# State-space stage: each slab's PSUM bank is copied to SBUF, and GpSimd's tap is added first

## The chip, the cores and the metric

The kernel runs on one core of a Trainium2 chip. The core has five engines with an instruction queue of its own each: TensorE (matrix products into PSUM), VectorE, ScalarE and GpSimd (elementwise work; GpSimd reads and writes SBUF alone here) and SyncE (starts the DMAs). An engine takes its instructions strictly in order, and semaphores hold an instruction until what it needs is done. The metric is the device time of one execution in microseconds; less is better.

## The reference

Two transformer-like blocks on a sequence of 256 tokens of width 1024 in float32. The first has a sparse-attention mixer and a state-space mixer (Mamba-2 style), each followed by a feed-forward layer with a causal convolution; the second has a gated delta rule with memory attention and a feed-forward layer. What the change touches is the state-space mixer's entry:

```python
proj = h @ w_in
z = proj[..., :SSD_D_INNER]
xbc = jax.nn.silu(causal_dwconv(proj[..., SSD_D_INNER:SSD_D_INNER + SSD_CONV_DIM], conv_w, conv_b))
...
y = ssd_scan(x_ssm, dt, a, bm, cm) + d_skip.astype(f32)[:, None] * x_ssm
y = y.reshape(b, s, SSD_D_INNER) * jax.nn.silu(z.astype(f32))
```

The convolution runs over positions, with four taps per channel and a bias; x (2048 channels), B and C (512 each) go through it, z (2048) does not.

## The kernel before, in words

The stages run one after the other: attention, feed-forward 0, state space, feed-forward 1, delta rule, feed-forward 2. Activations lie feature-major, 128 features on the partitions by 256 positions. A weight slab of 256 output features comes by two DMAs of 512 KB; each half is split into a high part (ScalarE, L361, whi) and a low part (VectorE or GpSimd, L362, wlo), and every product is three matmuls of such parts (L308). `up` gathers one slab's products in a PSUM bank of 128 x 512 numbers, two feature tiles of 256 positions (tag u, two banks; tag b, two more, serves all small products; four acc banks), and then calls that slab's `evac`.

The state-space stage has 20 slabs: B and C (two each), x (eight, x00 to x31) and z (eight). B0 and C0 are the two slabs that `enter` makes while it comes from the stage before; their results lie in acc banks. In this stage x.rb is None (the normalisation is already in the activations), so `scaled` (L744) hands on the bank itself. For B, C and x the evac is `convsilu`, which calls `conv` (L753): per feature tile c, ScalarE writes u = tap 3 times the bank plus bias (L762), and tap 2 times the bank to a scratch tile called tap (L764); VectorE adds taps 1 and 0 with a shift of two and three positions, each a scalar_tensor_tensor that reads the bank and u (L767); and GpSimd adds the scratch tile with a shift of one (L769). Then `silu2` (L771): th = tanh(u/2) on ScalarE (L773), out = (th + 1) u on VectorE (L774); the factor of two is taken out later. For z the evac is `gate`: silu2 of the bank itself.

TensorE's order is written by hand (the order of the Python code, with `fill` and `need` putting slabs between the small products of the scan). VectorE, ScalarE and GpSimd are ordered by a scheduler at build time from priorities; `high_priority(offset=URGENT // 2)` moves an instruction forward. At the entry `enter` transposes B0 and C0 back, and then `tails` makes the 32 dt columns: matmuls, a copy to SBUF by ScalarE (L681, tail), two transposes by TensorE; from them come dt, softplus (L781 to L792) and da. After that TensorE runs slabs z00, x00, x01, then the first small products of the scan: decay sums, ah (L1206), and per pair of heads dd (L1245), ee (L1247 to L1249), w (L1251) and x (L1261, which reads a b bank).

Of the kernel before, what the change touches and what calls it, by code (L numbers as in the profile page):

```python
# [10 lines left out]
F32 = mybir.dt.float32  # L11
# [7 lines left out]
P = 128  # L19
S = 256  # L20
# [12 lines left out]
URGENT = 2000  # L33
# [214 lines left out]
class Net:  # L248
# [492 lines left out]
            self.need("tail")  # L741
        return x

    def scaled(self, pool, ps, rb, tag="p", bufs=2):  # L744

        if rb is None:
            return ps.rearrange("p (c s) -> p c s", c=2)
        p = pool.tile([P, 2, S], F32, tag=tag, name=self.nm(tag), bufs=bufs)
        with self.tc.high_priority(offset=URGENT // 2):
            self.nc.vector.tensor_tensor(p, ps.rearrange("p (c s) -> p c s", c=2), rb[:, None, :].to_broadcast([P, 2, S]), op=ALU.mult)  # L750
        return p

    def conv(self, u, p, w, i, taps, bias=None, pool=None):  # L753

        nc = self.nc
        col = lambda c, t: self.pc(w, i[c] * taps + t)
        both = range(len(u))
        for c in both:
            if bias is None:
                nc.scalar.activation(u[c], p[c], AF.Copy, scale=col(c, taps - 1))  # L760
            else:
                nc.scalar.activation(u[c], p[c], AF.Identity, scale=col(c, taps - 1), bias=self.pc(bias, i[c]))  # L762
            if pool is not None:
                nc.scalar.activation(pool[c], p[c], AF.Copy, scale=col(c, taps - 2))  # L764
        for c in both:
            for sh in range(1 if pool is None else 2, taps):
                nc.vector.scalar_tensor_tensor(u[c][:, sh:], p[c][:, :S - sh], col(c, taps - 1 - sh), u[c][:, sh:], op0=ALU.mult, op1=ALU.add)  # L767
            if pool is not None:
                nc.gpsimd.tensor_add(u[c][:, 1:], u[c][:, 1:], pool[c][:, :S - 1])  # L769

    def silu2(self, out, u, th):  # L771

# [60 lines left out]


    def ffn(self, i, conv, left, gain_pre, mem=None):
        nc = self.nc
        with self.tc.tile_pool(name=f"ffn{i}", bufs=3) as fp:
# [304 lines left out]
    def ssd(self, left):  # L1142
        nc = self.nc
        mm = self.mm
        with self.tc.tile_pool(name="ssd", bufs=1) as sp:
            t = lambda s, shape, dt=F32, b=1: sp.tile(shape, dt, tag=s, name=self.nm(s), bufs=b)
            out = {}

            def convsilu(key, i, b=1):

                def evac(ps, x):
                    p = self.scaled(sp, ps, x.rb)
                    u, o = t("u", [P, 2, S], b=2), t(key if b == 1 else key[0], [P, 2, S], b=b)
                    pool = [self.np_.tile([P, S], F32, tag="sq", name=self.nm("tap"), bufs=3) for _ in range(2)]
                    self.conv((u[:, 0], u[:, 1]), (p[:, 0], p[:, 1]), "scw", (i, i + 1), 4, "scb", pool)
                    self.silu2(o, u, t("th", [P, 2, S], b=2))
                    out[key] = o
                return evac

            def gate(key):  # L1160
                def evac(ps, x):
                    u, o = self.scaled(sp, ps, x.rb), t("z", [P, 2, S], b=4)
                    self.silu2(o, u, t("th", [P, 2, S], b=2))
                    out[key] = o
                return evac

# [3 lines left out]
            x = self.enter(left, None, "gain10", "ssd_up", [convsilu("B0", 16), convsilu("C0", 20)], ("ssd_dt", 32),  # L1170
                           then=lambda x: (setattr(self, "pool_lo", POOL_E), self.add("z00", zs(0, 0, x))))
# [18 lines left out]
            ps = self.bank()  # L1190
# [10 lines left out]
            ps = self.bank()  # L1201
# [90 lines left out]
            for g in range(4):  # L1292
# [18 lines left out]
                for c in range(2):  # L1311
                    ps = self.bank()
# [599 lines left out]
```

## Time and profile before

| | |
|---|---|
| time before, median of 3 runs | 1330.9 us (1323.39 to 1338.49) |
| the profiled execution: time, span | 1329.81 us, 1328.0 us |
| TensorE busy, whole span | 1246.6 us (94%) |
| VectorE, ScalarE, GpSimd busy | 896.1, 715.9, 226.9 us |
| mean granted TensorE clock | 0.964 of full speed |

The profile is of one execution. In its rows PE is TensorE's matmuls and PEld its weight loads, DVE is VectorE, ACT ScalarE, POOL GpSimd. Times are us from the start of the span, and "out<-in" names the tiles; L is the line in the kernel. Consecutive instructions of an engine overlap by about 0.1 us in the rows. The waits are inferred from semaphore events: where several semaphores are awaited, the last counts.

### The profile page before, as it was taken

How to read it: one execution, taken by the hardware profiler on the slowest of the kernel's cores; microseconds unless marked ns; L12 is line 12 of the kernel's file. 1: busy time of each engine (PE TensorE's matmuls, PEld its weight loads, DVE VectorE, ACT ScalarE, POOL GpSimd, SP SyncE). 2: the span in 40 equal slices, each digit the busy share in tenths (PEclk: the TensorE clock that was granted, in tenths of full speed). 3: DMA queues.
4: the chain of work that ended last, by engine and by line, in shares of the span. 5: the costliest groups of instructions: out<-in, count | busy, mean ns of one | idle time of the engine just before them, and what ended most of it. 6: DMA issues, size and time to landing. Idle time of an engine off the chain costs nothing.

```text
span 1328.0 us, 22701 instructions
## 1 busy us (share of the span) xinstructions
PE 1246.6 (94%) x8874; PEld 1110.1 (84%) x8874; DVE 896.1 (67%) x1647; ACT 715.9 (54%) x1340; POOL 226.9 (17%) x149
## 2 busy tenths in 40 slices
PE   8999989999999989999899999998867999999997
PEld 8874579999988888877899998888867887999996
DVE  6776658877776677865798777577873335755554
ACT  6365547765556655544766655743423454744442
POOL 2000003110005322411211000350321332300000
PEclk9997999999999989989999999987878899999999
DMA  8740136655544334424455555342311114555551
GB/s 316 283 143 1 33 118 201 197 184 188 183 153 140 118 110 143 137 102 140 167 194 191 181 181 187 116 155 96 112 48 49 64 64 159 172 192 180 185 184 41
DMA packets 54108, 192.78 MB, mean 145 GB/s; under 512 B 6128, under 2 KB 6768, under 8 KB 53616
## 3 DMA queue, kind: packets, MB, share of 16 engines
q1 hardware_dynamic: 54000, 191.32, 43.2%
q8 instruction: 70, 1.15, 0.4%
q14 instruction: 38, 0.31, 0.1%
HBM read 190.25 MB, written 1.05 MB: 144 GB/s over the span
## 4 chain that ended last, share of the span: by engine, by line
PE 49%; DVE 9%; issue 7%; ACT 3%; POOL 2%; DMA 0%; POOLq 0%; DVEq 0%; ACTq 0%
PE u L308 29%; PE acc L308 16%; PE b L308 3%; DVE u L767 2%; DVE wlo L362 1%; ACT whi L361 1%; PE b L313 1%; POOL wlo L362 1%; POOL x L1267 0%; POOL rs L457 0%; DVE et L1698 0%; DVE rs L459 0%; POOL l2r L1585 0%; DMA raw<-in_gdn_up_dram 0%; ACT u L762 0%
## 5 line engine op out<-in xcount | busy, mean ns | idle before, releaser
L361 ACT ACTIVATE whi<-raw 128x1024 fp32r<-128x1024 f32 (+1 forms) x342 | 356.1, 1048 | 255.9 <-PE u L308 122.2
L308 PE MATMUL u<-xhi,whi 128*128 128x256 f32 x1600 | 467.0, 292 | 12.3 <-DVE xp L1628 5.5
L362 DVE TENSOR_TENSOR wlo<-raw,whi 128x1024 fp32r<-128x1024 f32 (+1 forms) x283 | 351.3, 1247 | 183.8 <-ACT whi L361 181.7
L308 PE MATMUL u<-xlo,whi 128*128 128x256 f32 x1600 | 458.7, 287 | 0.0
L308 PE MATMUL u<-xhi,wlo 128*128 128x256 f32 x1600 | 458.6, 287 | 0.0
L308 PEld LDWEIGHTS u<-xhi,whi 128*128 128x128 f32 x1600 | 313.2, 196 | 20.5 <-issue 15.4
L308 PEld LDWEIGHTS u<-xlo,whi 128*128 128x128 f32 x1600 | 313.3, 196 | 2.3
L308 PEld LDWEIGHTS u<-xhi,wlo 128*128 128x128 f32 x1600 | 312.8, 196 | 0.0
L362 POOL TENSOR_TENSOR wlo<-raw,whi 128x1024 fp32r<-128x1024 f32 x59 | 145.4, 2474 | 207.5 <-ACT whi L361 205.0
L308 PE MATMUL acc<-whi,yhi 128*128 128x512 f32 x376 | 150.9, 401 | 0.1
L308 PE MATMUL acc<-whi,ylo 128*128 128x512 f32 x376 | 149.8, 398 | 0.6 <-DVE ylo L362 0.6
L308 PE MATMUL acc<-wlo,yhi 128*128 128x512 f32 x376 | 149.8, 398 | 0.0
L574 POOL TENSOR_TENSOR post<-post,mhalf 128x1 f32<-128x1 f32 x12 | 6.5, 544 | 533.3 <-DVE post L573 523.2
L308 PEld LDWEIGHTS acc<-whi,ylo 128*128 128x128 f32 x376 | 71.1, 189 | 18.4 <-DVE ylo L362 1.0
L308 PEld LDWEIGHTS acc<-whi,yhi 128*128 128x128 f32 x376 | 71.4, 190 | 15.6 <-ACT yhi L361 0.6
L308 PEld LDWEIGHTS acc<-wlo,yhi 128*128 128x128 f32 x376 | 70.9, 189 | 14.3
L361 ACT ACTIVATE yhi<-y 128x256 fp32r<-128x256 f32 x66 | 27.2, 412 | 41.7 <-DVE y L851 41.6
L767 DVE SCALAR_TENSOR_TENSOR u<-u,par,u 128x254 f32<-128x254 f32 (+2 forms) x100 | 46.0, 473 | 5.1 <-ACT u L760 2.4
L535 DVE SCALAR_TENSOR_TENSOR xlo<-b,par,xhi 128x128 fp32r<-128x128 f32 x80 | 24.7, 345 | 29.8 <-ACT xhi L534 29.4
L767 DVE SCALAR_TENSOR_TENSOR uv<-p,par,uv 128x255 f32<-128x255 f32 x80 | 42.6, 532 | 0.1
L308 PE MATMUL acc<-whi,xhi 128*128 128x256 f32 x160 | 34.2, 295 | 8.9 <-ACT xhi L534 8.9
L534 ACT ACTIVATE xhi<-b,par 128x128 fp32r<-128x128 f32 x80 | 25.5, 366 | 31.5 <-PE b L313 28.4
(388 smaller groups left out, 1819.9 us busy)
## 6 DMA issues: line engine op xcount, KB each, us to landing
raw<-in_ffn_up_dram SPq DMA_DIRECT2D x132, 512.0 KB, 4.5
raw<-in_ffn_down_dram SPq DMA_DIRECT2D x66, 512.0 KB, 4.6
raw<-in_ssd_up_dram SPq DMA_DIRECT2D x40, 512.0 KB, 4.1
raw<-in_gdn_up_dram SPq DMA_DIRECT2D x36, 512.0 KB, 4.0
raw<-in_nsa_up_dram SPq DMA_DIRECT2D x16, 512.0 KB, 6.0
raw<-in_ssd_out_dram SPq DMA_DIRECT2D x16, 512.0 KB, 4.4
raw<-in_gdn_out_dram SPq DMA_DIRECT2D x12, 512.0 KB, 3.9
raw<-in_nsa_out_dram SPq DMA_DIRECT2D x8, 512.0 KB, 6.3
```

Source lines behind the costliest of these rows:

```text
L308: self.nc.tensor.matmul(out, lhsT, rhs, start=start, stop=stop, skip_group_check=True)
L313: self.nc.tensor.transpose(out, in_, self.c("ident", n)[:, :n])
L361: self.nc.scalar.activation(hi, src, AF.Copy)
L362: return (lo_engine or self.nc.vector).tensor_sub(lo, src, hi.bitcast(F32))
L534: act = nc.scalar.activation(h, ps, AF.Copy, scale=self.pc(gain, k))
L535: return act, nc.vector.scalar_tensor_tensor(l, ps, self.pc(gain, k), h.bitcast(F32), op0=ALU.mult, op1=ALU.subtract)
L574: nc.gpsimd.tensor_tensor(r[:, one], ms[:, one], self.mhalf, op=ALU.pow)
L767: nc.vector.scalar_tensor_tensor(u[c][:, sh:], p[c][:, :S - sh], col(c, taps - 1 - sh), u[c][:, sh:], op0=ALU.mult, op1=ALU.add)
```

## The change

`scaled` gets a way to copy: with copy=True and no rb, VectorE copies the bank of 128 x 512 numbers to an SBUF tile p (two buffers), at a raised priority. Both evacs of the state-space stage use it, so that all further reads of the slab, by ScalarE and VectorE, are of p. In `conv`, GpSimd's add comes ahead of VectorE's two taps in program order, and since all write u, VectorE's taps now follow GpSimd's add. The tile th goes away: tanh is written over p for B, C and x, and into a u buffer for z. `conv` is used with GpSimd's tap by this stage alone.

```diff
-    def scaled(self, pool, ps, rb, tag="p", bufs=2):
-
+    def scaled(self, pool, ps, rb, tag="p", bufs=2, copy=False):
+
+        if rb is None and copy:
+            p = pool.tile([P, 2, S], F32, tag=tag, name=self.nm(tag), bufs=bufs)
+            with self.tc.high_priority(offset=URGENT // 2):
+                self.nc.vector.tensor_copy(p, ps.rearrange("p (c s) -> p c s", c=2))
+            return p
         if rb is None:
...
             if pool is not None:
                 nc.scalar.activation(pool[c], p[c], AF.Copy, scale=col(c, taps - 2))
+            if pool is not None:
+                nc.gpsimd.tensor_add(u[c][:, 1:], u[c][:, 1:], pool[c][:, :S - 1])
         for c in both:
             for sh in range(1 if pool is None else 2, taps):
                 nc.vector.scalar_tensor_tensor(u[c][:, sh:], p[c][:, :S - sh], col(c, taps - 1 - sh), u[c][:, sh:], op0=ALU.mult, op1=ALU.add)
-            if pool is not None:
-                nc.gpsimd.tensor_add(u[c][:, 1:], u[c][:, 1:], pool[c][:, :S - 1])
...
-                    p = self.scaled(sp, ps, x.rb)
+                    p = self.scaled(sp, ps, x.rb, copy=True)
...
-                    self.silu2(o, u, t("th", [P, 2, S], b=2))
+                    self.silu2(o, u, p)
...
-                    u, o = self.scaled(sp, ps, x.rb), t("z", [P, 2, S], b=4)
-                    self.silu2(o, u, t("th", [P, 2, S], b=2))
+                    u, o = self.scaled(sp, ps, x.rb, copy=True), t("z", [P, 2, S], b=4)
+                    self.silu2(o, u, t("u", [P, 2, S], b=2))
```

The rows below are the instructions in the order in which they stand on an engine; the line numbers of the changed kernel are five higher from the middle of `conv` on (L762 is L767 there, L773 is L778).

ScalarE at the entry, before: B is u_4737 with bank acc_4732, C is u_4759 with bank acc_4754.

```order
L762 ACTIVATE u_4737<-acc_4732,par 128x256
L764 ACTIVATE tap_4739<-acc_4732,par 128x256
L762 ACTIVATE u_4737<-acc_4732,par 128x256
L764 ACTIVATE tap_4740<-acc_4732,par 128x256
L762 ACTIVATE u_4759<-acc_4754,par 128x256
L764 ACTIVATE tap_4761<-acc_4754,par 128x256
L762 ACTIVATE u_4759<-acc_4754,par 128x256
L681 ACTIVATE tail_4542<-acc_4716 32x256
L764 ACTIVATE tap_4762<-acc_4754,par 128x256
L773 ACTIVATE th_4751<-u_4737 128x512
```

The same place of the change, where the copies are p_4737 (B) and p_4760 (C):

```order
L767 ACTIVATE u_4739<-p_4737,par 128x256
L769 ACTIVATE tap_4741<-p_4737,par 128x256
L767 ACTIVATE u_4739<-p_4737,par 128x256
L769 ACTIVATE tap_4742<-p_4737,par 128x256
L767 ACTIVATE u_4762<-p_4760,par 128x256
L769 ACTIVATE tap_4764<-p_4760,par 128x256
L767 ACTIVATE u_4762<-p_4760,par 128x256
L778 ACTIVATE p_4737<-u_4739 128x512
L769 ACTIVATE tap_4765<-p_4760,par 128x256
L681 ACTIVATE tail_4542<-acc_4716 32x256
```

The tanh of B (L778) and one tap of C now stand ahead of tail, which stood ahead of both.

VectorE at the same place, before:

```order
L362 TENSOR_TENSOR wlo_4896<-raw_4893,whi_4895 128x1024
L362 TENSOR_TENSOR wlo_4968<-raw_4965,whi_4967 128x1024
L767 SCALAR_TENSOR_TENSOR u_4737<-acc_4732,par,u_4737 128x254
L767 SCALAR_TENSOR_TENSOR u_4737<-acc_4732,par,u_4737 128x253
L767 SCALAR_TENSOR_TENSOR u_4737<-acc_4732,par,u_4737 128x254
L767 SCALAR_TENSOR_TENSOR u_4737<-acc_4732,par,u_4737 128x253
```

And in the change:

```order
L362 TENSOR_TENSOR wlo_4900<-raw_4897,whi_4899 128x1024
L362 TENSOR_TENSOR wlo_4973<-raw_4970,whi_4972 128x1024
L749 COPY p_4737<-acc_4732 128x512
L749 COPY p_4760<-acc_4755 128x512
L774 SCALAR_TENSOR_TENSOR u_4739<-p_4737,par,u_4739 128x254
L774 SCALAR_TENSOR_TENSOR u_4739<-p_4737,par,u_4739 128x253
L774 SCALAR_TENSOR_TENSOR u_4739<-p_4737,par,u_4739 128x254
L774 SCALAR_TENSOR_TENSOR u_4739<-p_4737,par,u_4739 128x253
```

Both copies stand behind the two weight splits, and the taps read p.

GpSimd some 45 us later, from a weight split on, before (u_5253 and u_5352 are the slabs x10 and x11, the L1267 rows gate x00 and x01 with z):

```order
L362 TENSOR_TENSOR wlo_5498<-raw_5495,whi_5497 128x1024
L1267 TENSOR_TENSOR x_4949<-x_4949,z_4883 128x512
L769 TENSOR_TENSOR u_5253<-u_5253,tap_5255 128x255
L769 TENSOR_TENSOR u_5253<-u_5253,tap_5256 128x255
L769 TENSOR_TENSOR u_5352<-u_5352,tap_5354 128x255
L769 TENSOR_TENSOR u_5352<-u_5352,tap_5355 128x255
```

And in the change:

```order
L362 TENSOR_TENSOR wlo_5509<-raw_5506,whi_5508 128x1024
L771 TENSOR_TENSOR u_5262<-u_5262,tap_5264 128x255
L771 TENSOR_TENSOR u_5262<-u_5262,tap_5265 128x255
L1272 TENSOR_TENSOR x_4955<-x_4955,z_4887 128x512
L771 TENSOR_TENSOR u_5362<-u_5362,tap_5364 128x255
L771 TENSOR_TENSOR u_5362<-u_5362,tap_5365 128x255
```

The adds of x10 moved ahead of the gate and stand right behind the split; VectorE's taps of x10 follow them. TensorE's and SyncE's orders are the same in both kernels.

## Rows read from the trace of the kernel before

**Rows 1.** Busy time by engine in two stretches; columns as the first line says.
```profile
core 0: us, PE busy (x) PEld busy (x) DVE busy (x) ACT busy (x) POOL busy (x), PEclk, DMA share, GB/s
405.00:655.00 250.00, 227.64 (x1550) 201.04 (x1550) 174.85 (x285) 139.40 (x283) 74.04 (x54) 0.95 0.40 133
...
540.00:560.00 20.00, 20.00 (x165) 18.35 (x162) 18.39 (x32) 15.67 (x35) 6.50 (x6) 1.00 0.49 169
```

**Rows 2.** Waits of PE, 405 to 655: us in total, times, longest.
```profile
PE b L308 <- DVE rs L459: 7.2, 3, 2.9
PE b L308 <- DVE ah L1206: 2.8, 1, 2.8
...
PE b L308 <- DVE x L1261: 2.7, 1, 2.7
PE acc L313 <- ACT tail L681: 1.9, 1, 1.9
...
PE u L308 <- DVE u L767: 1.6, 1, 1.6
```

**Rows 3.** Waits of all engines, 400 to 660, same columns.
```profile
ACT whi L361 <- PE u L308: 25.4, 16, 8.3
```

**Rows 4.** Timeline of ACT at the entry: start, us, instruction, idle before it.
```profile
410.54 0.55 ACT L762 ACTIVATE u<-acc,par 128x256 f32<-128x256 f32 x1
...
412.15 0.58 ACT L762 ACTIVATE u<-acc,par 128x256 f32<-128x256 f32 x1
...
413.40 0.36 ACT L681 ACTIVATE tail<-acc 32x256 f32<-32x256 f32 x1
415.50 0.47 ACT L764 ACTIVATE tap<-acc,par 128x256 f32<-128x256 f32 x1 [1.75 <-POOL u L769]
416.19 0.63 ACT L773 ACTIVATE th<-u 128x512 f32<-128x512 f32 x1 [0.21 <-POOL u L769]
```

**Rows 5.** Timeline of DVE at the entry.
```profile
409.16 3.41 DVE L362 TENSOR_TENSOR wlo<-raw,whi 128x1024 fp32r<-128x1024 f32 x1
412.49 1.89 DVE L767 SCALAR_TENSOR_TENSOR u<-acc,par,u 128x254 f32<-128x254 f32 x4
...
423.47 2.89 DVE L774 SCALAR_TENSOR_TENSOR C<-th,u 128x512 f32<-128x512 f32 x1
```

**Rows 6.** Groups of DVE, 405 to 655: xcount | busy us, mean ns | idle before.
```profile
L570 DVE TENSOR_TENSOR t<-acc,gains 128x512 f32<-128x512 f32 x4 | 2.8, 690 | 2.7 <-ACT psq L562 2.6
```

**Rows 7.** Timeline of POOL at the entry and later.
```profile
411.44 3.35 POOL L362 TENSOR_TENSOR wlo<-raw,whi 128x1024 fp32r<-128x1024 f32 x1
414.75 1.41 POOL L769 TENSOR_TENSOR u<-u,tap 128x255 f32<-128x255 f32 x2
...
423.36 2.45 POOL L362 TENSOR_TENSOR wlo<-raw,whi 128x1024 fp32r<-128x1024 f32 x1 [3.38 <-ACT whi L361]
...
456.49 2.40 POOL L362 TENSOR_TENSOR wlo<-raw,whi 128x1024 fp32r<-128x1024 f32 x1 [5.09 <-ACT whi L361]
```

**Rows 8.** Stretches behind two waits of PE, columns as in rows 1.
```profile
416.00:420.00 4.00, 4.00 (x29) 4.00 (x28) 3.23 (x11) 0.78 (x2) 2.04 (x3) 0.77 0.77 276
...
1008.00:1012.00 4.00, 3.35 (x17) 3.35 (x18) 1.35 (x3) 0.49 (x1) 0.00 (x0) 0.53 0.00 0
```

**Rows 9.** Timeline of PE behind the longer wait, in the delta-rule stage.
```profile
1008.65 0.69 PE L313 MATMUL b<-cst,gpsq 128*128 128x128 f32 x2 [7.58 <-DVE gpsq L774]
```

**Rows 10.** Line L767: ns min/median/max, first and last start; state space, then feed-forward 0.
```profile
L767 DVE SCALAR_TENSOR_TENSOR u<-u,par,u x40: 464/473/483, 430.3 to 557.2; 128x254 f32<-128x254 f32 x20, 128x253 f32<-128x253 f32 x20
...
L767 DVE SCALAR_TENSOR_TENSOR uv<-p,par,uv x40: 470/478/2645, 211.9 to 369.9; 128x255 f32<-128x255 f32 x20, 128x254 f32<-128x254 f32 x20
```

**Rows 11.** Timeline of ACT at the tanh of x11 and z01.
```profile
471.01 1.11 ACT L773 ACTIVATE th<-u 128x512 f32<-128x512 f32 x2 [2.54 <-POOL u L769]
```

**Rows 12.** Line L762, columns as in rows 10.
```profile
L762 ACT ACTIVATE ug<-p,par x40: 590/602/607, 209.7 to 819.2; 128x256 f32<-128x256 f32 x40
L762 ACT ACTIVATE uv<-p,par x40: 585/587/591, 210.2 to 819.7; 128x256 f32<-128x256 f32 x40
L762 ACT ACTIVATE u<-u,par x20: 545/561/564, 428.2 to 553.3; 128x256 f32<-128x256 f32 x20
```

## What the change does to the time: the prediction

> **What bounds the kernel now.** I read the busy sums by stage first. The state-space stage lies between about 405 and 655 us of the span; there TensorE is busy 227.64 of 250 us, VectorE 174.85, ScalarE 139.40 and GpSimd 74.04 [rows 1]. The order of TensorE's instructions is the same before and after, instruction by instruction, so the change can only move TensorE's idle time: 22.4 us in this stage, and no more than that can be won (plus some clock, below). The second view is who TensorE waited for in that stretch [rows 2]. Three waits for VectorE's rs (7.2 us) come from the normalisation and do not touch the slabs. What the change can reach: 1.6 us for a PSUM bank (VectorE's tap u), 2.8 us for ah, 2.7 us for x, 1.9 us for ScalarE's tail. So the thing that the copy does directly, freeing the slab's bank earlier, is worth 1.6 us here. Weights are no concern: ScalarE waits 25.4 us for TensorE to give weight buffers back [rows 3], so weights are split as far ahead as their buffers allow.
>
> **The entry of the stage is where a term changes most.** TensorE transposes tail there and cannot go on without it. Before, ScalarE runs the four affine instructions of B from 410.54 to 412.15 (1.61 us for u, tap, u, tap), three of C until 413.40, then tail, done at 413.76 [rows 4]. In the changed order tail stands behind the tanh of B, and that tanh needs the whole of B's convolution. Step by step, with durations of the rows: VectorE's two weight splits ahead of the copies end at 409.16 + 3.41 = 412.57 [rows 5], unchanged. Copy of B: 0.69 us by the nearest row, VectorE's 128x512 read of acc [rows 6] (0.48 to 0.69 would move this by 0.2 at most), so 413.2. ScalarE's four: 413.2 + 1.6 = 414.8. GpSimd ends its weight splits at 411.44 + 3.35 = 414.79, and its two adds take 1.41 [rows 7], so 416.2. VectorE's four taps take 1.89 [rows 5]; the first pair can run beside the second add, so the last ends at 416.2 + 0.95 = 417.15. If C's add gets between them, up to two adds of 0.7 us more: 418.6. Then tanh, one tap of C and tail on ScalarE: 0.63 + 0.47 + 0.36 [rows 4], less about 0.2 by which neighbours overlap: 1.25. Tail is done at 418.4 to 419.85 instead of 413.76: **TensorE starts 4.6 to 6.1 us later, I take 5.3.** Nothing covers it: TensorE has no other work in its order. What stands behind tail on VectorE (softplus for da) is late by the same, and TensorE with it, so that it costs once.
>
> **The clock.** After a wait of 1.9 us at this place the stretch 416 to 420 ran at a granted clock of 0.77 [rows 8], part of it at 1.2 instead of 2.4 GHz: about 0.9 us lost. The nearest longer wait, 7.58 us for gpsq [rows 9], was followed by 0.53 in 1008 to 1012 [rows 8], 1.9 us lost. I add 0.5, bounds 0 and 1.
>
> **The copies and taps on VectorE.** 20 copies (4 B and C, 8 x, 8 z) by 0.69 are 13.8 us. The 48 taps read p in SBUF instead of PSUM. Alone that is the same price: the SBUF form uv<-p in the first feed-forward stage has a median of 478 ns, the PSUM form here 473 [rows 10]. But beside GpSimd it is not. The PSUM taps at 412.49 ran at their usual 0.47 each under a GpSimd split that lasted until 414.79 [rows 5, 7]; of the PSUM form the longest is 483 ns. The SBUF form's longest is 2645 [rows 10], and C<-th,u, which has two SBUF inputs, took 2.89 us at 423.47 while GpSimd's split of 423.36 lasted until 425.81 [rows 5, 7]. So a tap with two SBUF inputs waits until GpSimd's instruction ends. In the Trainium skill, "SBUF — State Buffer", section "Who interferes with whom", the rule is that a VectorE instruction with two SBUF inputs contends for a read interface shared with GpSimd and is shut out for the other's whole instruction; the rows agree, and by this rule the edit is a loss where GpSimd is busy. Against it, "VectorE: DVE Perf Modes", section "Rules for kernel authors", advises copying PSUM to SBUF first if many operations follow; with 478 against 473 ns the rows show no gain from that per tap.
>
> Price: GpSimd is busy 0.30 of the stage, in 54 pieces of 1.37 us on average [rows 1]. A tap that comes at random hits one 3 times in 10 and waits half of it: 48 x 0.30 x 0.69 = 9.9 us. Bounds: nothing if all miss, at most GpSimd's 74 us. VectorE rises from 174.85 to about 198.6 of 250 us. Most of it is covered by VectorE's idle time. The cover is thin where VectorE is already full: 540 to 560, 18.39 of 20 us; with some three copies (2.1) and a fifth of the tap waits (2.0) it would need 22.5 of 20 [rows 1]. I let 2 us reach TensorE (0 to 8).
>
> **GpSimd's add ahead of VectorE's taps.** It takes GpSimd out of the end of the chain: at 471.01 ScalarE's tanh had waited 2.54 us for GpSimd's add [rows 11], which delayed x and so the 2.7 us wait of TensorE. That wait was for the last of two adds, some 1.7 us after VectorE's last tap. On the other side VectorE's taps, and all that is queued behind them (x, w, dd), now wait when the add stands behind a weight split on GpSimd, such as the 2.40 us one at 456.49 [rows 7]: the changed order has that split ahead of two adds of a slab of x. Two copies (1.4 us) lie in the same stretch. I take -0.5 for this place (bounds -2.7 and +2). At ah the adds and copies come out even: ScalarE reaches ah earlier, but VectorE's silu of x stands ahead of it and meets GpSimd's split; 0 (bounds -2.8 and +1).
>
> **ScalarE** reads p at 587 to 602 ns instead of 561 from PSUM [rows 12]; 56 instructions, about 2 us, on an engine with 110 idle us: 0. The PSUM wait goes: -1.6. Buffers: p and u have two each, as u had, so slabs are no deeper in flight than before.
>
> **The sum.** 5.3 + 0.5 + 2 - 0.5 - 1.6 = +5.7. The profiled execution took 1329.81 us, 1.8 more than its span, and lies 1.1 below the median of 1330.9 of three runs that reach from 1323.39 to 1338.49. Forecast: 1335.5, which is 0.4% above it. A measurement of this kernel can tell about 1% (13 us) from no change, so this counts as the same.
>
> **The rivals.**
> - *The entry stall is as said, the rest small* (the forecast): 1330 to 1344, 0.62.
> - *The copies free more than they cost* (the other side): tail is not late, since GpSimd's splits there end early or ScalarE is not held, and the waits for the bank (1.6), ah (2.8), x (2.7) shrink to nothing, with the 1 to 3 us of low clock that followed them. 1329.8 - 7 - 3 = 1320. For it: the chain is a GpSimd link shorter at its end. Against it: the changed row order at the entry. It decides if tail is done before 413.76. 0.21, of which 0.04 go below 1317.6 (1% under the median).
> - *VectorE becomes the bound*: it is nearly full in 540 to 560, and a tap held up by GpSimd holds the mixing's x and w behind it. If half of 13.8 + 9.9 reaches TensorE, 5.8 + 12 - 2 = +16: 1346; all of it, 1357. Against it: 75 idle us and weights far ahead. 0.17; it decides from about 9 us of new waits for VectorE's w, x or dd.
>
> So faster by over 1%: 0.04; within: 0.80; slower: 0.16. The forecast's own range is 1330 to 1344; the range for 8 in 10 is 1324 to 1348, which takes in most of both rivals and half a per cent of scatter.
>
> **What would show it.** Right: TensorE's wait for tail at the entry is 6 to 8 us instead of 1.9; no wait of TensorE for a u bank; 20 copies of 0.5 to 0.7 us; taps with a median near 475 ns and some of 1 to 2.7 us; GpSimd no longer waiting for u, VectorE waiting for GpSimd's u instead. Wrong: a tail wait under 3 us; or new waits for w, x or dd that together pass 9 us.

## The result and the profile after

The changed kernel takes 1336.45 us, the median of 20 runs (1329.12 to 1349.27), against 1331.18 us of 20 runs of the kernel before. The ratio is 1.0069 with a 95% interval of [1.0044, 1.0093]: some 0.7% longer, under the 1% that counts as a difference here. The two medians as they stand differ by less, 5.27 us or 0.4%; the ratios and intervals of this document compare the fast runs alone, without, among others, four runs of 1738 to 3000 us (one each of the kernel before, copy_only, before_tail and entry_plain). The forecast was 1335.5 us and "the same". The profiled execution took 1333.46 us, with this page:

```profile
span 1331.7 us, 22717 instructions
...
PE 1244.9 (93%) x8874; PEld 1108.7 (83%) x8874; DVE 912.0 (68%) x1667; ACT 718.8 (54%) x1340; POOL 232.0 (17%) x149
```

The stage by stretches, after (columns as the first line says), beside [rows 1]:

```profile
core 0: us, PE busy (x) PEld busy (x) DVE busy (x) ACT busy (x) POOL busy (x), PEclk, DMA share, GB/s
405.00:655.00 250.00, 223.50 (x1510) 197.99 (x1510) 186.86 (x300) 135.31 (x271) 75.96 (x52) 0.92 0.38 127
441.00:541.00 100.00, 92.10 (x641) 82.33 (x642) 75.49 (x120) 58.19 (x118) 32.40 (x24) 0.91 0.36 116
470.00:490.00 20.00, 16.34 (x100) 15.04 (x99) 13.43 (x22) 9.11 (x21) 6.09 (x5) 0.74 0.24 79
500.00:520.00 20.00, 18.14 (x148) 16.79 (x148) 19.34 (x27) 12.60 (x27) 9.60 (x6) 1.00 0.39 134
510.00:530.00 20.00, 17.39 (x97) 13.94 (x95) 16.57 (x23) 10.74 (x21) 6.00 (x4) 0.83 0.42 139
```

VectorE has 12.0 us more to do in these 250 us (186.86 for 174.85), TensorE is busy 4.1 us less, and the mean granted clock is 0.92 for 0.95. Who TensorE waits for, after, beside [rows 2]; us in total, times, longest:

```profile
PE acc L313 <- ACT tail L681: 7.7, 1, 7.7
PE b L308 <- DVE rs L459: 7.2, 3, 2.9
PE b L308 <- DVE x L1266: 3.4, 3, 1.9
PE b L308 <- DVE w L1256: 3.1, 2, 2.3
...
PE b L308 <- DVE ah L1211: 1.4, 1, 1.4
```

The wait for tail grew from 1.9 to 7.7 us. The wait for a PSUM bank is gone, ah's fell from 2.8 to 1.4, x and w together rose from 3.3 to 6.5, and rs is what it was. The entry after, first ScalarE, then VectorE, then GpSimd (start, us, instruction, idle before it), beside [rows 4, 5, 7]; the VectorE and GpSimd rows go on to a second place, at 515 us:

```profile
412.49 0.60 ACT L767 ACTIVATE u<-p,par 128x256 f32<-128x256 f32 x1 [2.58 <-DVE p L749]
...
417.57 0.63 ACT L778 ACTIVATE p<-u 128x512 f32<-128x512 f32 x1 [1.80 <-DVE u L774]
418.10 0.49 ACT L769 ACTIVATE tap<-p,par 128x256 f32<-128x256 f32 x1
418.50 0.36 ACT L681 ACTIVATE tail<-acc 32x256 f32<-32x256 f32 x1
```

```profile
411.78 1.27 DVE L749 COPY p<-acc 128x512 f32<-128x512 f32 x2
414.78 3.61 DVE L774 SCALAR_TENSOR_TENSOR u<-p,par,u 128x254 f32<-128x254 f32 x6 [1.72 <-POOL u L771]
...
516.61 2.51 DVE L779 SCALAR_TENSOR_TENSOR C<-p,u 128x512 f32<-128x512 f32 x1
519.04 0.47 DVE L1266 SCALAR_TENSOR_TENSOR x<-x,dsk,b 128x256 f32<-128x256 f32 x1
519.43 0.68 DVE L779 SCALAR_TENSOR_TENSOR z<-u,p 128x512 f32<-128x512 f32 x1
520.03 0.94 DVE L1256 TENSOR_TENSOR w<-ee,cb 128x768 f32<-128x768 f32 x1
```

```profile
402.70 11.36 POOL L362 TENSOR_TENSOR wlo<-raw,whi 128x1024 fp32r<-128x1024 f32 x4 [15.88 <-ACT whi L361]
414.02 2.26 POOL L771 TENSOR_TENSOR u<-u,tap 128x255 f32<-128x255 f32 x3
...
516.19 2.38 POOL L362 TENSOR_TENSOR wlo<-raw,whi 128x1024 fp32r<-128x1024 f32 x1 [4.48 <-ACT whi L361]
```

Tail is done at 418.86, behind the tanh of B (L778), as the prediction's chain said. At 515 us VectorE comes to the silu of C while GpSimd's split of 516.19 runs, and takes 2.51 us for what takes 0.69 elsewhere. Behind it in VectorE's order stand x (L1266) and w (L1256), and TensorE waits for both, as the rows of TensorE show (the third and fourth of these); the rest are places at which all kernels can be compared:

```profile
418.91 0.42 PE L313 MATMUL acc<-cst,tail 32*128 32x32 f32 x2 [7.67 <-ACT tail L681]
442.05 0.50 PE L308 MATMUL b<-ah,sel 64*128 64x256 f32 x2 [1.39 <-DVE ah L1211]
...
519.56 0.50 PE L308 MATMUL b<-ah,sel 64*128 64x256 f32 x2 [1.85 <-DVE x L1266]
521.03 1.55 PE L308 MATMUL b<-w,xdt 128*64 128x256 f32 x8 [0.76 <-DVE w L1256]
...
545.24 0.68 PE L308 MATMUL b<-cst,rs 128*128 128x128 f32 x4 [2.15 <-DVE rs L459]
...
641.44 0.63 PE L313 MATMUL b<-cst,h 128*128 128x128 f32 x4 [1.93 <-DVE h L580]
```

The same four places of the kernel before:

```profile
413.81 0.31 PE L313 MATMUL acc<-cst,tail 32*128 32x32 f32 x2 [1.89 <-ACT tail L681]
437.46 0.50 PE L308 MATMUL b<-ah,sel 64*128 64x256 f32 x2 [2.75 <-DVE ah L1206]
...
537.67 0.68 PE L308 MATMUL b<-cst,rs 128*128 128x128 f32 x4 [2.15 <-DVE rs L459]
...
635.43 0.63 PE L313 MATMUL b<-cst,h 128*128 128x128 f32 x4 [1.63 <-DVE h L580]
```

Since TensorE's order is the same in all these kernels, the time between two such rows is a measure of the stretch. I count from where TensorE falls idle for tail (the row's start less its wait: 411.92 before, 411.24 after) to ah, from ah to the first rs, and on to h. That gives 25.54, 100.21 and 97.76 us before (sum 223.5), and 30.81, 103.19 and 96.20 after (sum 230.2). **The stage is 6.7 us longer: 5.3 at the entry, 3.0 in the middle, 1.6 shorter at the end.** The spans differ by less, 3.7 us: the stage began 0.7 us earlier, and the stages behind it, which the change does not touch, ran 2.3 us shorter in this execution.

Every kernel that was run, by the same rows (us; "x, w" holds xdt too, and "traced" is the time of the execution that was profiled). Each ratio is to runs of the kernel before on the same chip, whose medians were 1331.18 for the changed kernel, 1329.31 for the four below it, 1329.73 for the next four, 1328.15 for three and 1328.26 for the last:

| kernel | tail | ah | bank | x, w | to ah | ah to rs | rs to h | stage | traced | time | ratio, 95% |
|---|---|---|---|---|---|---|---|---|---|---|---|
| before | 1.89 | 2.75 | 1.58 | 4.4 | 25.5 | 100.2 | 97.8 | 223.5 | 1329.81 | | 1 |
| changed | 7.67 | 1.39 | 0 | 6.9 | 30.8 | 103.2 | 96.2 | 230.2 | 1333.46 | 1336.45 | 1.0069 [1.0044, 1.0093] |
| reorder_only | 4.30 | 4.22 | 1.49 | 1.0 | 29.3 | 95.1 | 96.3 | 220.6 | 1327.21 | 1327.27 | 0.9990 [0.9960, 1.0021] |
| copy_only | 7.23 | 1.23 | 0 | 6.2 | 30.4 | 100.5 | 96.5 | 227.4 | 1330.66 | 1335.77 | 1.0031 [0.9997, 1.0065] |
| after_tail | 2.57 | 5.13 | 0 | 7.2 | 28.5 | 102.8 | 98.9 | 230.2 | 1336.70 | 1335.10 | 1.0066 [1.0030, 1.0102] |
| before_tail | 0.71 | 2.75 | 4.97 | 3.6 | 26.4 | 97.8 | 96.3 | 220.5 | 1327.37 | 1327.47 | 0.9961 [0.9925, 0.9998] |
| copies_unread | 4.91 | 1.14 | 5.62 | 2.9 | 27.8 | 100.6 | 99.2 | 227.7 | 1332.85 | 1334.03 | 1.0069 [1.0036, 1.0101] |
| taps_from_bank | 6.48 | 1.14 | 6.48 | 1.2 | 29.5 | 98.2 | 100.9 | 228.6 | 1336.49 | 1334.51 | 1.0059 [1.0027, 1.0090] |
| no_z_copy | 7.69 | 1.39 | 0 | 5.9 | 30.7 | 101.1 | 97.8 | 229.5 | 1333.37 | 1331.65 | 1.0013 [0.9979, 1.0047] |
| reorder_tail | 0.65 | 4.46 | 3.77 | 1.0 | 27.0 | 94.1 | 96.2 | 217.3 | 1322.23 | 1325.42 | 0.9979 [0.9947, 1.0011] |
| scalar_copy | 7.66 | 1.34 | 0 | 5.8 | 29.8 | 98.4 | 96.3 | 224.5 | 1328.55 | 1328.00 | 1.0014 [0.9977, 1.0052] |
| z_copy_only | 4.31 | 4.22 | 2.55 | 2.9 | 30.6 | 98.7 | 94.7 | 224.0 | 1334.93 | 1333.47 | 1.0045 [1.0007, 1.0082] |
| entry_plain | 4.32 | 3.57 | 0 | 6.4 | 29.5 | 104.3 | 96.2 | 230.0 | 1333.48 | 1334.37 | 1.0060 [1.0025, 1.0095] |
| scalar_entry_tail | 0.72 | 4.26 | 0 | 5.8 | 24.3 | 99.9 | 93.3 | 217.4 | 1318.33 | 1323.24 | 0.9960 [0.9933, 0.9987] |

The waits and stretches are each of one profiled execution, the times medians of several runs. A traced execution need not be a middling one: that of scalar_entry_tail is the shortest of its 12, and that of copy_only lies 5.1 us under its median, so that differences of a few us between stages need the times beside them. The next sections go through them by question.

### The profile page after: what moved, and what is told of

Read it like the earlier page. It is cut to its first block, busy times and chain, and to the rows that moved or that the text cites. A ratio compares the mean times of both kernels' runs of the same rounds, so it can differ in the third digit from the quotient of the medians.

```text
span 1331.7 us, 22717 instructions
## 1 busy us (share of the span) xinstructions
PE 1244.9 (93%) x8874; PEld 1108.7 (83%) x8874; DVE 912.0 (68%) x1667; ACT 718.8 (54%) x1340; POOL 232.0 (17%) x149
## 4 chain that ended last, share of the span: by engine, by line
PE 47%; DVE 11%; issue 7%; ACT 3%; POOL 2%; POOLq 0%; DVEq 0%; ACTq 0%
PE u L308 26%; PE acc L308 17%; PE b L308 3%; DVE u L774 3%; DVE wlo L362 2%; ACT whi L361 1%; PE b L313 1%; POOL u L771 0%; DVE p L749 0%; POOL wlo L362 0%; ACT xhi L534 0%; POOL rs L457 0%; DVE et L1703 0%; DVE rs L459 0%; POOL l2r L1590 0%
## 5 line engine op out<-in xcount | busy, mean ns | idle before, releaser
L362 POOL TENSOR_TENSOR wlo<-raw,whi 128x1024 fp32r<-128x1024 f32 x59 | 149.2, 2537 | 209.9 <-ACT whi L361 207.5
L535 DVE SCALAR_TENSOR_TENSOR xlo<-b,par,xhi 128x128 fp32r<-128x128 f32 x80 | 24.7, 345 | 29.8 <-ACT xhi L534 29.4
L1051 ACT ACTIVATE p<-acc,mx,r 128x128 f32<-128x128 f32 (+1 forms) x64 | 31.9, 510 | 19.2 <-DVE mx L1048 17.4
```

Source lines behind the costliest of these rows:

```text
L362: return (lo_engine or self.nc.vector).tensor_sub(lo, src, hi.bitcast(F32))
L535: return act, nc.vector.scalar_tensor_tensor(l, ps, self.pc(gain, k), h.bitcast(F32), op0=ALU.mult, op1=ALU.subtract)
L1051: nc.scalar.activation(p[:, b, :], s3[:, b, :], AF.Exp, scale=r8[:, qt:qt + 1], bias=mx[:, b:b + 1], accum_out=den[:, b:b + 1])
```

## Experiments: each half of the change alone

**reorder_only**: the kernel before with GpSimd's add ahead of VectorE's taps, and no copies. Its edit, like all that follow, is shown against the changed kernel.

```diff
-                    p = self.scaled(sp, ps, x.rb, copy=True)
+                    p = self.scaled(sp, ps, x.rb)
...
-                    u, o = self.scaled(sp, ps, x.rb, copy=True), t("z", [P, 2, S], b=4)
+                    u, o = self.scaled(sp, ps, x.rb), t("z", [P, 2, S], b=4)
...
```

Expected: 

> GpSimd's add ahead of VectorE's taps, which go on reading the PSUM bank; no copies. In this order one tap of C stands ahead of tail, and it waits for a scratch buffer that GpSimd's first add gives back (415.5 before). Entry theory: the wait for tail is about 4.5 us (2.6 more than before), and the rest gains a little, since tanh need not wait for GpSimd at the end of the chain: -0.1% to +0.3%. Load theory: no copies and no held-up taps, so the time is that of before, and the wait for a PSUM bank (1.6 us) stays.

**copy_only**: the copies, with GpSimd's add left behind VectorE's taps.

```diff
-            if pool is not None:
-                nc.gpsimd.tensor_add(u[c][:, 1:], u[c][:, 1:], pool[c][:, :S - 1])
         for c in both:
             for sh in range(1 if pool is None else 2, taps):
...
+            if pool is not None:
+                nc.gpsimd.tensor_add(u[c][:, 1:], u[c][:, 1:], pool[c][:, :S - 1])
```

Expected: 

> The copies to SBUF, with GpSimd's add left behind VectorE's taps as in the kernel before. Entry theory: tail stands behind B's tanh here too, the wait is 7 to 8 us and the time +0.4% to +0.9%, as with both parts. Load theory: the taps now run when their data are there, without waiting for GpSimd's add, so VectorE has less to wait for: +0.2% to +0.5%.

Measured: 0.9990 and 1.0031, and 1.0069 with both. reorder_only, waits of TensorE in the stage (us, times, longest):

```profile
PE acc L313 <- ACT tail L681: 4.3, 1, 4.3
PE b L308 <- DVE ah L1211: 4.2, 1, 4.2
...
PE u L308 <- DVE u L774: 1.5, 1, 1.5
PE b L308 <- DVE x L1266: 0.7, 1, 0.7
```

and its clock around 470 us:

```profile
470.00:490.00 20.00, 18.48 (x152) 17.43 (x151) 15.78 (x26) 11.21 (x24) 6.57 (x6) 1.00 0.37 119
```

The new order alone costs 3.7 us to ah, and gains 5.2 between ah and rs: x's wait of 2.7 us, which [rows 11] put down to GpSimd's add, falls to 0.7, and the clock in 470 to 490 is 1.00. The kernel before has 0.83 there (the second row is for a place that comes later):

```profile
470.00:490.00 20.00, 16.12 (x105) 15.51 (x106) 10.38 (x15) 8.05 (x16) 5.30 (x4) 0.83 0.23 74
510.00:530.00 20.00, 20.00 (x124) 16.47 (x122) 11.85 (x18) 11.81 (x25) 5.66 (x3) 1.00 0.48 158
```

Of the 3.7 us that the order alone costs, 2.4 are at tail: in reorder_only's trace one tap of C stands ahead of it on ScalarE, idle for 1.8 us until GpSimd's add is done. Another 1.5 are at ah: ahead of it VectorE is idle for 3.2 us until GpSimd's add of x01 is done, which stands behind a weight split (436.31 to 438.65). The tanh of B stands behind tail there, and ahead of it in copy_only, so each half puts something of its own ahead of tail.

The copies alone cost 4.8 us to ah and nothing on balance behind it (100.5 for 100.2). With both, the order's gain is gone: 103.2 between ah and rs, 8.1 us more than with the order alone. So the two halves don't add up. The explanation that the experiments below test is that the order wins only while VectorE has time to use it, and that the copies take this time.

## Experiments: the entry

**after_tail** and **before_tail**: the tail's ScalarE copy goes ahead of what waits on ScalarE, in this stage alone; the one on the changed kernel, the other on the kernel before.

```diff
-            nc.scalar.activation(flat, ps[:n, :S], AF.Copy)
+            if self.stage == 2:
+                with self.tc.high_priority(offset=URGENT):
+                    nc.scalar.activation(flat, ps[:n, :S], AF.Copy)
+            else:
+                nc.scalar.activation(flat, ps[:n, :S], AF.Copy)
```

Expected of after_tail: 

> The changed kernel, with ScalarE's copy of the dt columns (tail) at a raised priority in this stage alone, so that it stands behind the first two instructions of B instead of behind B's tanh. Entry theory (the loss is TensorE's wait for tail): the wait falls from 7.7 us to about 2, the low clock behind it from 5.7 to 3.4 us, and the time from +0.7% to within 0.3% of the kernel before. Load theory (the loss is VectorE's copies and held-up taps all through the stage, and the entry's wait is made up later): the wait falls too, but the waits for w and x grow, and the time stays at +0.4% to +0.8%.

Expected of before_tail: 

> The kernel before, with tail at the same raised priority; nothing else. It moves ahead of three instructions of C. Both theories: the wait for tail falls from 1.9 us to about 0.6, the low clock of 3.4 us behind it may go, 1 to 3 us less (-0.1% to -0.2%), below what the comparison can tell. If the time falls by over 0.5%, the entry weighs more than either theory says.

In after_tail the wait moved:

```profile
PE b L308 <- DVE ah L1215: 5.1, 1, 5.1
...
PE acc L313 <- ACT tail L683: 2.6, 1, 2.6
```

7.67 + 1.39 became 2.57 + 5.13. TensorE reached ah 2.3 us sooner, and the 2.3 us were lost again by h (230.2 and 230.2 for the stage), between rs and h, where nothing of this edit lies (98.9 for 96.2 us): no wait is longer there, but the granted clock is 0.86 in 542 to 567, where the changed kernel has 1.00 in 545 to 567. The time is unchanged, 1.0066, while the waits for x, w and xdt hardly grew (7.2 for 6.9 us), so neither theory came out whole. Why ah was late shows in what stands just ahead of it, the silu of the first x slab on VectorE, beside GpSimd's weight split; after_tail, then the changed kernel:

```profile
436.66 2.81 DVE L783 SCALAR_TENSOR_TENSOR x<-p,u 128x512 f32<-128x512 f32 x1
...
436.57 2.35 POOL L362 TENSOR_TENSOR wlo<-raw,whi 128x1024 fp32r<-128x1024 f32 x1 [2.94 <-ACT whi L361]
...
440.86 0.68 DVE L779 SCALAR_TENSOR_TENSOR x<-p,u 128x512 f32<-128x512 f32 x1
```

In after_tail the silu begins 0.1 us behind the split and takes 2.81 us instead of 0.68, which is 2.1 of the 5.1 us of ah's wait. In the changed kernel the split's row begins at 440.84, and the silu passes. So the time won at tail was partly lost where VectorE, now earlier, met GpSimd. In before_tail the same edit took 1.2 us of the tail wait and gave a bank wait of 3.4 us (VectorE's z) in its place. It measured 0.9961 with an interval that ends at 0.9998, and gained its 2.5 us between ah and rs, not at the entry.

**entry_plain**: the two slabs of the entry, B0 and C0, are read from their acc banks; the other 18 copies stay.

```diff
-                    p = self.scaled(sp, ps, x.rb, copy=True)
+                    p = self.scaled(sp, ps, x.rb, copy=key not in ("B0", "C0"))
...
-                    self.silu2(o, u, p)
+                    self.silu2(o, u, p if key not in ("B0", "C0") else t("p", [P, 2, S], b=2))
```

Expected: 

> The changed kernel with the two copies of the entry's slabs (B and C, in the acc banks) undone; the other 18 stay. If the wait for the tail is GpSimd's add being early (ScalarE's tanh of B then stands ahead of the tail), it stays at 4 to 7.7 us, since the kernel with the add moved and no copy waits 4.3 and the copies add what the chain of B lasts longer; and the time stays within 3 us of the changed kernel's, 1333 to 1337. If the entry's own copies make the wait, it falls to under 4.5 us and the time by some 3 us to about 1332.

Measured: the tail wait is 4.32 us, that of reorder_only (4.30). So of the 5.8 us by which the wait grew, the order makes 2.4 and the entry's two copies 3.3 on top. The bound for "the entry's own copies make the wait" (under 4.5) is met, but not its time: 1.0060, and a stage of 230.0 us. ah's wait rose to 3.57, behind the same silu, which takes 2.81 us here too, beside the GpSimd split of 437.83; the 1.3 us that were won to ah even so went between ah and rs.

## Experiments: is it the copying, or the reading of the copies?

**copies_unread**: the 20 copies are made, and everything reads the PSUM bank as before.

```diff
                     p = self.scaled(sp, ps, x.rb, copy=True)
+                    v = ps.rearrange("p (c s) -> p c s", c=2) if x.rb is None else p
...
-                    self.conv((u[:, 0], u[:, 1]), (p[:, 0], p[:, 1]), "scw", (i, i + 1), 4, "scb", pool)
+                    self.conv((u[:, 0], u[:, 1]), (v[:, 0], v[:, 1]), "scw", (i, i + 1), 4, "scb", pool)
...
-                    u, o = self.scaled(sp, ps, x.rb, copy=True), t("z", [P, 2, S], b=4)
+                    p, o = self.scaled(sp, ps, x.rb, copy=True), t("z", [P, 2, S], b=4)
+                    u = ps.rearrange("p (c s) -> p c s", c=2) if x.rb is None else p
```

Expected: 

> The changed kernel with the 20 copies made but read by no one: ScalarE, GpSimd's tap and VectorE's taps read the PSUM bank as in the kernel before; GpSimd's add stays ahead of VectorE's taps. If VectorE's load is what costs (20 x 0.68 = 13.6 us in the stage), the new waits of TensorE for x and w at 515 to 520 us (1.9 and 0.8 us in the changed kernel) stay, and the time is the changed kernel's, 1334 to 1337, ratio 1.003 to 1.007. If reading the copies costs (the taps on SBUF that GpSimd holds up, ScalarE's 0.6 instead of 0.56 us), those waits are gone and the time is that of the add alone, 1326 to 1330, ratio 0.997 to 1.001. In both the wait for a PSUM bank (1.5 us at 500) is back, since the bank is held until the last tap.

**taps_from_bank**: only VectorE's 48 taps read the bank; the rest reads the copy.

```diff
-                nc.vector.scalar_tensor_tensor(u[c][:, sh:], p[c][:, :S - sh], col(c, taps - 1 - sh), u[c][:, sh:], op0=ALU.mult, op1=ALU.add)
+                nc.vector.scalar_tensor_tensor(u[c][:, sh:], (v or p)[c][:, :S - sh], col(c, taps - 1 - sh), u[c][:, sh:], op0=ALU.mult, op1=ALU.add)
...
```

Expected: 

> The changed kernel with one thing undone: VectorE's 48 taps read the PSUM bank; ScalarE's three readings and the gate's read the copy. If the taps' reading of SBUF beside GpSimd is what costs, the longest tap falls from 1.51 us to under 0.6, the new waits at 515 to 520 us go, and the time falls by 4 to 6 us to about 1330. If VectorE's load costs, the waits for x and w stay within 1 us of 2.6 in sum and the time stays at 1334 to 1337.

Measured: 1.0069 and 1.0059, the changed kernel's time. VectorE's groups in the stage (xcount | busy us, mean ns | idle before), first the changed kernel:

```profile
L774 DVE SCALAR_TENSOR_TENSOR u<-p,par,u 128x254 f32<-128x254 f32 (+1 forms) x48 | 26.9, 588 | 9.9 <-POOL u L771 9.5
...
L749 DVE COPY p<-u 128x512 f32<-128x512 f32 x18 | 12.3, 683 | 0.6 <-PE u L308 0.6
```

then copies_unread:

```profile
L774 DVE SCALAR_TENSOR_TENSOR u<-u,par,u 128x254 f32<-128x254 f32 (+1 forms) x40 | 18.4, 476 | 3.5 <-POOL u L771 3.0
L749 DVE COPY p<-u 128x512 f32<-128x512 f32 x18 | 12.3, 686 | 2.7 <-PE u L308 2.7
```

Reading the SBUF copy makes a tap 588 ns on average for 473 in [rows 10], 48 x 0.115 = 5.5 us in all, and this vanishes with the PSUM source. The time stays. The waits for x and w at 515 to 520 did go, against what the load theory expected there; but the banks, held until the last tap again, came free later than ever. The waits of TensorE in copies_unread have

```profile
PE u L308 <- DVE u L774: 5.6, 2, 4.2
```

for the 1.6 us of [rows 2]. VectorE, 12 us fuller, is late with whatever is asked of it next: x and w in one kernel, the last tap that frees a bank in the other. The copying by itself is enough for the whole loss: copies_unread differs from reorder_only in 20 copies that nothing reads (and in the tiles that the tanhs are written to), and it measured 1.0069 for 0.9990, with a stage of 227.7 for 220.6 us. That the reading is free is not shown: against the changed kernel the waits for x, w and xdt fell by 4.0 us in copies_unread and 5.7 in taps_from_bank, and the waits for banks rose by 5.6 and 6.5, so a price of the reading and the gain of a bank freed early may cancel. Nor is the hold-up by GpSimd gone in copies_unread: w takes 22.1 us there for 18.3 in reorder_only, and the x silus 8.5 for 5.5, so 6.8 us more fall on instructions whose inputs lie in SBUF in every kernel.

## Experiments: whose load, and which copies?

**scalar_copy**: the same 20 copies, made by ScalarE.

```diff
-                self.nc.vector.tensor_copy(p, ps.rearrange("p (c s) -> p c s", c=2))
+                self.nc.scalar.activation(p, ps.rearrange("p (c s) -> p c s", c=2), AF.Copy)
```

Expected: 

> The changed kernel with its 20 copies made by ScalarE instead of VectorE; who reads them is unchanged. ScalarE is busy 135 of the stage's 250 us and would get some 20 x 0.6 = 12 us. If it is VectorE's load that costs, the waits of TensorE for VectorE's x and w at 515 to 520 us (2.6 us in the changed kernel) go and the time falls by 4 us or more, to 1326 to 1331, ratio under 1.002. If it is the extra link in each slab's chain (the copy ahead of the taps) or the taps' reading of SBUF, whoever copies, the time stays at 1334 to 1338, ratio 1.004 to 1.008.

Measured: 1.0014, 1328.0 us. Stretches of scalar_copy:

```profile
405.00:655.00 250.00, 223.25 (x1542) 198.32 (x1541) 174.25 (x284) 149.97 (x300) 71.69 (x54) 0.95 0.39 132
441.00:541.00 100.00, 91.05 (x662) 82.31 (x663) 73.78 (x112) 62.45 (x128) 33.18 (x26) 0.97 0.35 116
510.00:530.00 20.00, 17.43 (x108) 14.28 (x107) 13.77 (x23) 12.99 (x29) 5.33 (x3) 1.00 0.48 161
```

and its taps:

```profile
L774 DVE SCALAR_TENSOR_TENSOR u<-p,par,u 128x254 f32<-128x254 f32 (+1 forms) x48 | 29.2, 628 | 13.4 <-POOL u L771 12.9
```

VectorE is back at 174.25 us, ScalarE is up by 14.7, and ah to rs takes 98.4 instead of 103.2 us, though the taps read SBUF and are held up by GpSimd even more (628 ns). The entry, with the chain of links unchanged, is as late as in the changed kernel (7.66). That parts the two: the entry is the chain's length, and 4.8 us of the middle go with VectorE's load. The middle is still 3.3 us longer than with the order alone (95.1), with 5.8 us of waits for x, w and xdt instead of 1.0; whether the extra link in each slab's chain, the taps' SBUF sources or ScalarE's load makes this, no run separates. One expectation missed: the waits for w around 515 to 525 did not go (0.79 and 1.78 us, in sum the 2.6 us of the changed kernel). What differs there is the clock, 1.00 for 0.83 in 510 to 530, and 0.97 for 0.91 in 441 to 541. Of the 4.8 us 1.1 is wait (5.8 for 6.9 us of x, w and xdt), and the other 3.7 go with the clock. The intervals of the two ratios still overlap by 0.0008, so these two times alone would not settle it. The others go with it: the six kernels with 18 or 20 copies on VectorE lie at 1.0031 to 1.0069, and the five with none there at 0.9960 to 1.0014.

**no_z_copy**: the gate's 8 copies undone; **z_copy_only**: only those 8 kept, on reorder_only.

```diff
-                    u, o = self.scaled(sp, ps, x.rb, copy=True), t("z", [P, 2, S], b=4)
+                    u, o = self.scaled(sp, ps, x.rb), t("z", [P, 2, S], b=4)
```

```diff
-                    p = self.scaled(sp, ps, x.rb, copy=True)
+                    p = self.scaled(sp, ps, x.rb)
...
```

Expected of no_z_copy: 

> The changed kernel with the 8 copies of the gate slabs undone (they read the PSUM bank as before), the 12 copies of the convolved slabs kept: 8 x 0.68 = 5.5 us less of VectorE's work. If VectorE's load costs, in proportion to it, 40% of the copies' price comes back (2 of about 5 us): about 1334, and the waits at 515 to 520 us shrink by half or more. If reading the copies costs, the taps are unchanged (longest near 1.5 us) and the time stays at 1335 to 1337.

Expected of z_copy_only: 

> The changed kernel with only the 8 copies of the gate slabs kept; the 12 convolved slabs are read from the PSUM bank. 8 x 0.68 = 5.5 us of VectorE's work against the kernel with GpSimd's add moved and no copy (ratio 0.999). By the load of VectorE in proportion, 40% of the 10 us between that kernel and the changed one: 1331 to 1332, ratio 1.000 to 1.004. If the gate's copies carry most of the price, as the times of the kernel without them (1.0013 against 1.0069) say, 1333 to 1336, 1.004 to 1.007. If they cost nothing, as the trace of the kernel without them says (its stage is as long as the changed kernel's), 1327 to 1329, 0.997 to 1.000.

Measured: 1.0013 for 12 copies, 1.0045 for the other 8, between 0.9990 for none and 1.0069 for all. By the traces it is the other way about: the stage takes 229.5 us with the 12 and 224.0 with the 8, between 220.6 and 230.2. The intervals are 0.003 wide to each side, and a trace is one execution, so which copies cost more stays open. The trace of z_copy_only took 1334.93 us with a stage of the length of before, because the stage began at 419.01, 7.1 us later than before, behind stages that no edit touches. In both the place at 515 us is met again: in no_z_copy C passes in 0.68 us, and w, whose two inputs lie in SBUF too, takes 1.88 for 0.94 beside GpSimd's split, and TensorE waits 1.89 for it; in z_copy_only C takes 2.35 us, and TensorE does not wait.

## Experiments: better than both

**reorder_tail**: reorder_only with the tail's edit of before_tail. **scalar_entry_tail**: the edits of scalar_copy, entry_plain and after_tail together.

Expected of reorder_tail: 

> The kernel before with two edits and no copies: GpSimd's add ahead of VectorE's taps, and the tail's ScalarE copy put ahead of what waits there in this stage. Each alone measured 0.999 and 0.996. If the two gain in different places (GpSimd's order in the stretch 445 to 490, the tail at 411), their sum is 0.993 to 0.997, 1322 to 1326 us. If both draw on the same slack, it is no better than 0.996 to 0.999, 1325 to 1330; the wait for the tail should be under 2 us in both, and ah's takes its place (4 to 5 us) in the second.

Expected of scalar_entry_tail: 

> The changed kernel with the three losses that the runs so far name taken away: the 18 copies of the u banks made by ScalarE, the two entry slabs read from their acc banks, and the tail's copy put ahead of what waits on ScalarE in this stage. If the losses were the entry (3.4 us by 445 us) and VectorE's load (4.4 us between 445 and 545), the sum of the waits for the tail and for ah is 7.4 us or less (0.7 and 4.5, as with the add moved and the tail raised alone), no wait for a u bank at 500, and the time is 1321 to 1327, ratio 0.994 to 0.999. If ScalarE, at some 150 of 250 us, gives the gain back by late weight splits or late tails, it is 1328 to 1332, ratio 1.000 to 1.003.

Measured: 0.9979, no difference that the runs can tell; and 0.9960 [0.9933, 0.9987], 1323.24 us, shorter than the kernel before by 0.4%. Its waits of TensorE have

```profile
PE b L308 <- DVE ah L1215: 4.3, 1, 4.3
PE b L308 <- DVE w L1260: 4.0, 3, 1.8
...
PE acc L313 <- ACT tail L683: 0.7, 1, 0.7
```

tail and ah 5.0 us together (9.1 in the changed kernel) and none for a bank. With the load on ScalarE the entry's edits keep what they win: to ah 24.3 us for scalar_copy's 29.8, stage 217.4 for 224.5, where the same two edits, each by itself on the changed kernel, won no time. The silu of the first x slab, at 431.89, is ahead of GpSimd's split of 432.39 here and takes 0.68 us. This trace is of the shortest of the 12 runs, 4.9 us under their median, so a part of the 7.1 us is the execution's; the two medians, on different chips, lie 4.8 us apart. The two together with the copies left on VectorE were not run, so that it needs ScalarE's copies is not shown. ScalarE, at 155 of 250 us, gave none of it back that shows. Nor do the copies win time here that shows: before_tail, with one edit and no copy, measured 0.9961 as well, with a wider interval.

## Why the prediction was right, and where it was not

The sum was +5.7 us and the stage came out 6.7 longer, the ratio 0.7% of 1330 = 9 us longer, with an interval from 6 to 12 (the medians, 5.3 us). The forecast of 1335.5 us and the class held. Term by term:

- **Entry, +5.3 (4.6 to 6.1): right in mechanism and size.** Tail was done at 418.86, inside 418.4 to 419.85 (also with the 0.7 us added by which the stage began earlier), and the wait grew by 7.67 - 1.89 = 5.8 us. It did not part the two halves of the change: the order alone makes 2.4 us, the copies alone 5.3 (7.23 in copy_only). And "Nothing covers it" left out that the next wait shrinks: ah fell by 1.4 us, so that ah's term of 0 was a gain of 1.4, inside its bounds (-2.8 to +1). That gain had luck in it: the silu of x that the prediction saw meeting GpSimd's split ahead of ah passed in the changed kernel, where the two rows begin 0.02 us apart, and was held up by 2.1 us in after_tail and entry_plain.
- **Clock, +0.5 (0 to 1)**: to ah the stretch grew by 5.27 us, where the two waits make 5.78 - 1.36 = 4.42, so 0.85 is left for it. The rows fit: behind tail TensorE's matmuls of 128x256 take 0.41 us instead of 0.28 until 417.8 before, some 3.5 us long, and from 419.3 to 424.5 after, some 5.2. The mean over the stage, 0.92 for 0.95, and 0.74 and 0.83 in the stretches of 470 and 510, show that the term was needed at more places than the one.
- **Bank wait, -1.6: right.** No wait for a bank is left in the changed kernel.
- **GpSimd's add ahead, -0.5 (-2.7 to +2): mis-sized.** Alone it is worth -5.2 us between ah and rs, outside the bounds (and costs 3.7 up to ah), since with the wait for x the low clock behind it went as well, and that was counted in a rival and not here.
- **VectorE, +2 (0 to 8): the step that failed.** The price of the pieces was too high: taps held up 5.5 us for 9.9, VectorE 186.86 us for 198.6. What reached TensorE was too low: with the order in place the copies make ah to rs 8.1 us longer, though they take 1.5 us of bank wait out of it, so 9.6, past the upper bound; 5.9 of that are waits for x, w and xdt (6.9 for 1.0). With the copies on ScalarE 4.8 of it went; what makes the rest is open. It was looked for in 540 to 560, the fullest window before, and came as waits for w and x at 472 to 478 (2.3 and 1.0 us) and at 515 to 521 (1.9 and 0.8), where VectorE is now full (19.34 us of 20 in 500 to 520), with low clock behind both. The hold-up by GpSimd was priced for the taps and took its toll elsewhere: scalar_copy, whose taps wait still longer, has the shorter middle, while one silu of C that waits 1.8 us ahead of x and w is paid by TensorE.
- **ScalarE, 0**: not told apart by any run.

The errors of order (-4.7) and load (+7.6) have opposite signs and cancel to +2.9, and the stretch from rs to h, for which nothing was forecast, took 1.6 off it, as in six of the other twelve kernels (96.2 to 96.5 us for 97.8); the total was close partly for that reason. The rival that the copies free more than they cost falls with the tail wait. The rival that VectorE becomes the bound named the right engine, but its mark, 9 us of new waits for x and w, is not reached: 6.5 for 3.3 us. By its own list, the tail wait of 6 to 8 us, the missing bank wait, copies of 0.67 to 0.69 us, and a median tap of 479 ns came as said, and the longest tap was 1.5 us, of the 1 to 2.7 that were forecast. GpSimd's waits for VectorE's u, 32.2 us in the stage before, are gone, and VectorE now waits for GpSimd's u, 9.5 us in nine places.

## What to carry to other kernels

Before work is added to an engine with idle time, look at the instructions of it that another engine waits for, and at what would stand ahead of them then: a mean of 70% busy hid windows that the new work filled. A copy that frees a buffer early is worth no more than the wait for that buffer (1.6 us here), and belongs to an engine whose next results others don't wait for: the same 20 copies cost 4.8 us less in the middle of the stage on ScalarE. A wait that is cured alone may only move: the entry's edits won no time one by one, and 5.5 us to ah together, with the copies on ScalarE. In two of them a part moved to a meeting of VectorE with GpSimd, for which a shift of 0.1 us was enough.

## What the runs showed of the hardware

- A VectorE instruction with two SBUF inputs stood until GpSimd's instruction ended: C's silu, begun at 516.61, ended at 519.12, where GpSimd's split ran from 516.19 to 518.57; it takes 0.69 us without one. The Trainium skill, "SBUF — State Buffer", section "Who interferes with whom", says that such an instruction contends with one of GpSimd that reads SBUF, and that the one that issues first locks the other out; the trace agrees. It does so in the other direction too: in the changed kernel the silu of 440.86 took its 0.68 us, and the GpSimd split whose row begins at 440.84 took 2.94 us instead of 2.40, so that there, it seems, GpSimd was the one held. In scalar_copy the mean tap (628 ns) shows it again.
- Two pairs of short waits of the same sum were followed by different clocks. In the changed kernel 1.85 and 0.76 us around 518 to 521 stand in a stretch (510 to 530) at a granted 0.83, part of it at 1.2 instead of 2.4 GHz; in scalar_copy 0.79 and 1.78 us around 516 to 525 stand in one at 1.00. Both came twice: entry_plain has 1.99 and 0.68 us, again 1.5 us apart, and 0.83; scalar_entry_tail 0.79 and 1.78, again 8.5 us apart, and 1.00. So the price of a wait was not a function of its length alone, and in the comparison of these two it is larger than the difference of the waits.
- ScalarE's copy of a 128x512 bank took 0.58 us (median of 18), VectorE's 0.68.
